# The first scan's values and gate columns become one product behind each row tile's transposes

## The chip, the cores and the metric

The kernel runs on one core of a Trainium2 chip. A core has a matrix engine (TensorE, PE in the profile, with its weight loads as PEld), a vector engine (VectorE, DVE), a scalar engine (ScalarE, ACT), a general one (GpSimd, POOL) and a queue engine (SyncE, SP) that issues the transfers here. The metric is the device time of one execution in microseconds. Three executions of the kernel before took 2996.06, 2998.18 and 3002.55 us, so the median is 2998.18. The profiled execution took 2996.87 us, and its span from the first to the last instruction is 2995.1 us.

## The reference

All arrays are fp32, with 1024 tokens of width 1024. A first block has two layers of the same form, each with three branches: a gated scan with four heads (GLA), a differential attention and a second gated scan (HGRN). A second block follows, with a neighbourhood attention and a delta rule; of it only small edits are touched. What the change touches in a layer is this.

```python
h = rms_norm(x, norm_pre[layer])
proj = h @ w_in[layer]
(gq, gk, gv, gg, gaf, gab, ...) = jnp.split(proj, offs, axis=-1)
# gla_branch:
v = split_heads(gv, GLA_HEADS)
lg_f = split_heads(jax.nn.log_sigmoid(gaf @ wa2_f + ba_f) / GLA_GATE_TEMP, GLA_HEADS)
lg_b = split_heads(jax.nn.log_sigmoid(gab @ wa2_b + ba_b) / GLA_GATE_TEMP, GLA_HEADS)
o = bidir_scan(q, k, k, v, lg_f, lg_b)
o = rms_norm(o, norm_w)
return merge_heads(o) * jax.nn.silu(g)
```

gq, gk are columns 0 to 255 of the projection, gv columns 256 to 511, gg 512 to 767, and gaf with gab the 32 columns 768 to 799.

## The kernel before

The tokens lie in 8 row tiles of 128. A product in fp32 is made of three products of fp32r parts: `split` gives H = the rounded value (a copy on ACT) and L = the rest (a subtraction, on VectorE unless another engine is named). So every product comes as HH, HL, LH over 8 blocks of the inner dimension: 24 matmuls an output tile.

A layer (`layer`, line 497 on) starts with its rows. In layer 0 each tile is loaded as x, squared on ACT with the sum (L307), gets its factor on GpSimd (L282, L283) and is multiplied by factor and norm row on VectorE (L312) into hn; in layer 1 the normed rows hn are loaded as they are. `transpose_split` (L287) turns each tile by 8 transposes in two PSUM tiles (tps) and splits it into hH and hL, which stay for the layer, as [channel, token].

Projections come in two forms. `proj_cm` is channel-major: weights are the stationary operand, 512 tokens the moving one, and the result has channels on its rows. `proj_tm` is token-major: a row tile's 128 tokens are stationary, the weights' columns move. Both write PSUM tiles pj, of which there are two. Weights come in pairs of 128 rows through two buffers wr and are split into wH, wL. Row tiles, channel-major results and gates live in ten buffers with the tag "in".

Projections are generators in a `Filler`, a list in the order in which they are due: gates (gf), queries and keys (gqk), values (gv), output gates (gg), and so on. `need` runs the list until a result is there; `run` steps a main computation and after each step gives the list a credit (RATE, in us), for which it emits matmuls beside it. Emission is also at a lower priority, and a scheduler lays out every engine's order when the program is built; each engine then works strictly in its order. SP's order is laid out in the same way, and at most 8 transfers are outstanding: an issue waits for the eighth before it.

The first scan needs gf and gqk. In `gla_gates` (L550) the 32 gate columns are projected channel-major (48 matmuls 32x512) into aT, multiplied with a small matrix (tile z), and go through Abs, Exp, Ln and Exp on ACT into the decay f. `scan_levels` (L340) forms running products of f, products psb and then six levels psl; `scan_finish` uses the values v. Constants of all stages are loaded early, the delta rule's bias dnb (dn_A_log, dn_dt_bias; L1275, L1286) too.

## Time and profile before

| what | us |
|---|---|
| median of three executions | 2998.18 |
| profiled execution | 2996.87 |
| its span | 2995.1 |
| TensorE busy | 2751.5 (92%) |
| VectorE busy | 1891.6 (63%) |
| ScalarE busy | 1228.9 (41%) |
| GpSimd busy | 555.2 (19%) |

A busy share is an average over stages with different limits. Where TensorE's share is below that of its neighbours, the timeline with its idle times says what it waited for. Matmuls overlap, so a step between two starts is what one costs, and not its listed duration. The granted clock of TensorE is 1.00 at 2.4 GHz and 0.5 at 1.2 GHz.

### The profile page before, as it was taken

The numbers are of one execution on the slowest core, as the hardware profiler recorded it, in microseconds if no ns is written. First come the engines' busy times: TensorE is split into PE (matmuls) and PEld (weight loads), VectorE is DVE, ScalarE is ACT, GpSimd is POOL, SyncE is SP. The second block draws the span as 40 slices with busy tenths as digits, with TensorE's granted clock in tenths as the row PEclk, the third lists the DMA queues.
The fourth block names the chain that finished last, engine by engine and source line by source line (L and its number), as shares of the span: only waits on it lengthen the run. The fifth ranks groups of instructions, "written<-read, shape, count | busy, mean of one in ns | idle before, by whom it ended". The sixth has DMA issues, their size and how long they took to land. (4 is left out here: it accounts for less than half of the span.)

```text
span 2995.1 us, 55723 instructions
## 1 busy us (share of the span) xinstructions
PE 2751.5 (92%) x21790; PEld 2342.9 (78%) x21790; DVE 1891.6 (63%) x4111; ACT 1228.9 (41%) x2729; POOL 555.2 (19%) x682
## 2 busy tenths in 40 slices
PE   7899889998999998899979899998899899989999
PEld 4788778896868886788968779875776677769889
DVE  4668777767546687766675645767686744346661
ACT  4232234556433322345564443433444433345430
POOL 1001212212100012222121212411422110010042
PEclk9999989998999998899989999998999999989999
DMA  3111122314331111223245534352435261255463
GB/s 112 29 43 36 41 79 79 94 48 120 128 142 30 44 36 41 78 80 102 53 132 160 180 88 135 119 137 57 132 107 145 78 172 45 71 151 149 145 206 97
DMA packets 355887, 293.61 MB, mean 98 GB/s; under 512 B 145798, under 2 KB 303110, under 8 KB 355624
## 3 DMA queue, kind: packets, MB, share of 16 engines
q1 hardware_dynamic: 355624, 290.04, 33.5%
q8 instruction: 172, 2.82, 0.4%
...
## 5 line engine op out<-in xcount | busy, mean ns | idle before, releaser
L163 DVE TENSOR_TENSOR wL<-wr,wH 128x512 fp32r<-128x512 f32 (+1 forms) x259 | 188.4, 733 | 216.5 <-ACT wH L162 213.5
L234 PE MATMUL pj<-wH,hH 128*128 128x256 f32 x1024 | 297.2, 292 | 14.8 <-ACT wH L162 8.5
L234 PE MATMUL pj<-wL,hH 128*128 128x256 f32 x1024 | 296.0, 290 | 1.2 <-DVE wL L163 1.2
L234 PE MATMUL pj<-wH,hL 128*128 128x256 f32 x1024 | 293.6, 288 | 0.0
L162 ACT CAST wH<-wr 128x512 fp32r<-128x512 f32 (+1 forms) x259 | 159.3, 618 | 277.8 <-PE pj L234 167.4
L234 PE MATMUL pj<-H,wH 128*128 128x512 f32 (+1 forms) x592 | 243.9, 414 | 8.8 <-DVE naz L1624 4.5
L234 PE MATMUL pj<-L,wH 128*128 128x512 f32 (+1 forms) x592 | 244.6, 413 | 0.0
L234 PE MATMUL pj<-H,wL 128*128 128x512 f32 (+1 forms) x592 | 244.5, 413 | 0.0
L234 PE MATMUL pj<-hH,wH 128*128 128x512 f32 (+1 forms) x544 | 221.5, 408 | 9.5 <-ACT raw L780 5.6
L234 PE MATMUL pj<-hL,wH 128*128 128x512 f32 (+1 forms) x544 | 222.3, 409 | 0.0
L282 POOL TENSOR_SCALAR rs<-ss 128x1 f32<-128x1 f32 (+2 forms) x190 | 68.9, 362 | 824.8 <-ACT sq L842 353.8
L234 PE MATMUL pj<-hH,wL 128*128 128x512 f32 (+1 forms) x544 | 221.5, 407 | 0.0
L234 PEld LDWEIGHTS pj<-wH,hH 128*128 128x128 f32 x1024 | 197.1, 193 | 20.6 <-ACT wH L162 9.9
L234 PEld LDWEIGHTS pj<-wL,hH 128*128 128x128 f32 x1024 | 197.6, 193 | 5.6 <-DVE wL L163 2.0
L234 PEld LDWEIGHTS pj<-wH,hL 128*128 128x128 f32 x1024 | 197.2, 193 | 2.6 <-issue 0.2
L814 DVE TENSOR_REDUCE nm<-psc 128x1 f32<-128x1024 f32 x128 | 155.6, 1219 | 43.1 <-PE psc L812 42.9
L817 ACT ACTIVATE p<-psc,nm 128x1024 f32<-128x1024 f32 x128 | 142.9, 1116 | 59.4 <-DVE nm L814 36.5
L283 POOL TENSOR_TENSOR rs<-rs,mhalf 128x1 f32<-128x1 f32 (+2 forms) x190 | 147.7, 778 | 15.3
L234 PEld LDWEIGHTS pj<-H,wH 128*128 128x128 f32 (+1 forms) x592 | 112.6, 190 | 35.8 <-DVE naz L1624 4.9
L839 PEld LDWEIGHTS pav<-v,wT 128*128 128x128 f32 x1024 | 132.0, 198 | 10.6 <-ACT wT L835 3.7
L839 PE MATMUL pav<-v,wT 128*128 128x128 f32 x1024 | 136.0, 282 | 2.5 <-ACT wT L835 2.0
L234 PEld LDWEIGHTS pj<-hH,wH 128*128 128x128 f32 (+1 forms) x544 | 101.8, 187 | 40.5 <-ACT raw L780 6.8
...
## 6 DMA issues: line engine op xcount, KB each, us to landing
...
xs<-raw SPq DMA_DIRECT2D x128, 64.0 KB
...
```

The costliest lines, as they stand in the source:

```text
L162: nc.scalar.copy(H, raw)
L163: (leng or nc.vector).tensor_tensor(L, raw, H.bitcast(F32), ALU.subtract)
L234: mm = k.nc.tensor.matmul(ps, x, y, start=i == 0, stop=i == len(terms) - 1)
L282: nc.gpsimd.tensor_scalar(r, ssq, scale, EPS, ALU.mult, ALU.add)
L283: nc.gpsimd.tensor_tensor(r, r, k.mhalf[:, :n], ALU.pow)
L814: nc.vector.tensor_reduce(nm, ps, axis=AX.X, op=ALU.max, negate=True)
L817: nc.scalar.activation(p, ps, AF.Exp, bias=nm, accum_out=z)
L839: k.mark = nc.tensor.matmul(po[:, :P], wT[:, kt, :], v[kt][:, vc0:vc0 + P], start=kt == 0, stop=kt == KT - 1)
```

## The change

The values and the gate columns of the first scan come from one token-major product with 288 columns, emitted right behind each row tile's transposes. Its weights sit in a new class that uses three buffers each of the tags "in" (low parts jL) and "be" (high parts jH). The result's 256 columns are copied to v, its 32 to ga; after four tiles four small transposes (tile aps) and a copy give half of aT. `gla_gates` is run directly, and no longer part of the list. In layer 0 rows are normed in place, and the squares go to a scratch tile jn. Constants' loads, and the first VectorE instruction on some of them, get an order-only dependency on the last weight load (lastw) or the last split of rows (lastL). The credit ahead of the first scan goes from 25.6 to 3.0. Several elementwise instructions move from GpSimd to VectorE, and one copy (sysA) from GpSimd to ACT.

```diff
@@ class Weights @@
-            nc.sync.dma_start(raw, src[i * P:(i + per) * P, :].rearrange(...))
+            k.lastw = nc.sync.dma_start(raw, src[i * P:(i + per) * P, :].rearrange(...))
+class JointWeights:
+    def __init__(self, k, src, n, src2, n2):
+        self.n = n + n2
+        self.L = [k.wk.tile([P, 3, self.n], F32R, tag="in", name="jL") for _ in range(3)]
+        self.H = [k.wk.tile([P, 3, self.n], F32R, tag="be", name="jH") for _ in range(3)]
+        raw2 = k.wp.tile([P, KT, n2], F32, tag="wr", name="wr")
+        nc.sync.dma_start(raw2, src2.rearrange("(k p) n -> p k n", p=P))
+        for i in range(3):
+            m = min(3, KT - 3 * i)
+            split(k, raw2[:, 3 * i:3 * i + m], self.H[i][:, 0:m, n:], self.L[i][:, 0:m, n:])
+        for k0 in range(0, KT, 2):
+            raw = k.wp.tile([P, 2, n], F32, tag="wr", name="wr")
+            k.lastw = nc.sync.dma_start(raw, src[k0 * P:(k0 + 2) * P, :].rearrange("(k p) n -> p k n", p=P))
+            ...
@@ transpose_split, behind, prenorm @@
-        nc.vector.tensor_tensor(L, pv, H.bitcast(F32), ALU.subtract)
+        k.lastL = nc.vector.tensor_tensor(L, pv, H.bitcast(F32), ALU.subtract)
+def behind(k, inst, mark):
+    info = mybir.DependencyInfo(mybir.DependencyClass.NoSync, mybir.DependencyReason.DATA)
+    k.tc.add_manual_dep(inst.ins, mark.ins.name, info, reason=...)
+    return inst
-    h = k.wk.tile([P, D], F32, tag="in", name="hn")
+    jk = k.wk.tile([P, D], F32, tag="at", name="jn")
-    nc.scalar.activation(h, x, AF.Square, accum_out=ss)
+    nc.scalar.activation(jk, x, AF.Square, accum_out=ss)
-        nc.vector.scalar_tensor_tensor(h, x, r, row, ALU.mult, ALU.mult)
+    nc.vector.scalar_tensor_tensor(x, x, r, row, ALU.mult, ALU.mult)
@@ scan_levels @@
-        nc.gpsimd.tensor_tensor(p0[:, :, 0, :], pf[:, :, 0, :], pb[:, :, 0, :], ALU.add)
-        nc.gpsimd.tensor_tensor(p1[:, :, 1, :], pf[:, :, 1, :], pb[:, :, 1, :], ALU.add)
+        nc.vector.tensor_tensor(p0[:, :, 0, :], pf[:, :, 0, :], pb[:, :, 0, :], ALU.add)
+        nc.vector.tensor_tensor(p1[:, :, 1, :], pf[:, :, 1, :], pb[:, :, 1, :], ALU.add)
@@ layer @@
-RATE = {"pre": 25.6, "gla": 4.95, ...}
+RATE = {"pre": 3.0, "gla": 4.95, ...}
+    def load_row(tt): ...
+    if l == 0:
+        load_row(0)
+        row = row_bcast(k, a["norm_pre"][l], D, k.wk, "in")
+        load_row(1)
+    Wv = JointWeights(k, w_in[:, 256:512], 256, w_in[:, 768:800], 32)
+    while len(hn) < NT:
+        load_row(len(hn))
+    ...
     for tt in range(NT):
+        if l == 0:
+            prenorm(k, hn[tt], row)
         transpose_split(k, hn[tt], tt // 4, tt % 4)
+        k.tc.cur_priority += RATE["low"]
+        ps = now(proj_tm(k, Wv, tt))
+        v = k.wk.tile([P, 256], F32, tag="v", name="v")
+        nc.scalar.copy(v, ps[:, 0:256])
+        gla_v.append(v)
+        ...
+        nc.scalar.copy(ga[:, tt % 4, :], ps[:, 256:288])
+        if tt % 4 == 3:
+            pt = k.sm.tile([P, 512], F32, tag="sm", name="aps")
+            for j in range(4):
+                nc.tensor.transpose(pt[:32, j * P:(j + 1) * P], ga[:, j, :], k.ident)
+            nc.scalar.copy(aT[:, tt // 4 * 512:tt // 4 * 512 + 512], pt[:32, :])
+        k.tc.cur_priority -= RATE["low"]
@@ gla_gates @@
-        Wa = Weights(k, w_in[:, 768:800], 32)
-        for half in range(2):
-            ps = yield from proj_cm(k, Wa, 0, 32, half)
-            nc.scalar.copy(aT[:, half * 512:half * 512 + 512], ps[:32, :])
@@ list and scan @@
-    F.add("gf", gla_gates())
-    F.add("gv", values(256))
-    fs = F.need("gf")
+    fs = gla_gates()
-    v, sg = F.need("gv"), F.need("gg")
+    v, sg = gla_v, F.need("gg")
@@ constants: every one in this form; lvlmask, bd4, bd2, lq, lk, lg, sc, modb, nw, nwc, rcos, rsin, wa, ba @@
-    nc.sync.dma_start(k.bd4, a["bd4"])
+    behind(k, nc.sync.dma_start(k.bd4, a["bd4"]), k.lastw)
-    nc.vector.tensor_scalar(th, th, 0.5, 0.5, ALU.mult, ALU.add)
+    behind(k, nc.vector.tensor_scalar(th, th, 0.5, 0.5, ALU.mult, ALU.add), k.lastL)
@@ second block @@
-        split(k, h.rearrange(...) if i == 0 else hv, H, L, nc.gpsimd if kt % 2 else nc.vector)
+        split(k, h.rearrange(...) if i == 0 else hv, H, L)
-    nc.gpsimd.tensor_copy(A, R.rearrange("s c r -> s r c"))
+    nc.scalar.copy(A, R.rearrange("s c r -> s r c"))
-        nc.gpsimd.tensor_tensor(e, e, D_.qT, ALU.mult)
+        nc.vector.tensor_tensor(e, e, D_.qT, ALU.mult)
-    nc.gpsimd.tensor_tensor(zv, zv, oT.rearrange(...), ALU.mult)
+    nc.vector.tensor_tensor(zv, zv, oT.rearrange(...), ALU.mult)
-    split(k, t, H, L, k.nc.gpsimd if c % 2 else k.nc.vector)
+    split(k, t, H, L)
-                nc.gpsimd.tensor_tensor(t, t, ut[:, hs], ALU.add)
+                nc.vector.tensor_tensor(t, t, ut[:, hs], ALU.add)
```

How the change moves the engines' orders is shown at three places. First TensorE at the very start of layer 0, in the kernel before; tps are a tile's transposes from the row tile hn, pj_311 is the gate columns' product:

```order
L294 MATMUL tps_188<-ident_60,hn_114 128x128 x4
L294 MATMUL tps_195<-ident_60,hn_114 128x128 x4
L294 MATMUL tps_202<-ident_60,hn_123 128x128 x4
L294 MATMUL tps_209<-ident_60,hn_123 128x128 x4
L294 MATMUL tps_216<-ident_60,hn_132 128x128 x4
L294 MATMUL tps_223<-ident_60,hn_132 128x128 x4
L294 MATMUL tps_230<-ident_60,hn_141 128x128 x4
L234 MATMUL pj_311<-hH_184,wH_306 32x512
L294 MATMUL tps_237<-ident_60,hn_141 128x128 x4
```

And in the changed kernel, where pj_186 is the first row tile's product with 288 columns:

```order
L320 MATMUL tps_172<-ident_60,hn_110 128x128 x4
L320 MATMUL tps_179<-ident_60,hn_110 128x128 x4
L260 MATMUL pj_186<-jH_119,hH_160 128x288
L260 MATMUL pj_186<-jL_116,hH_160 128x288
L320 MATMUL tps_222<-ident_60,hn_114 128x128 x4
L260 MATMUL pj_186<-jH_119,hL_162 128x288
L260 MATMUL pj_186<-jH_119,hH_160 128x288
L260 MATMUL pj_186<-jL_116,hH_160 128x288
L260 MATMUL pj_186<-jH_119,hL_162 128x288
L320 MATMUL tps_229<-ident_60,hn_114 128x128 x4
```

All tiles' transposes stood ahead of nearly all products; now the products of a tile stand between the transposes of the next ones.

Second, ACT between the casts of layer 0's first row tiles, in the kernel before; hn are the Squares (L307), hH_184 the casts of tiles 0 to 3, scth the Tanh of sc:

```order
L298 CAST hH_184<-tps_202 128x4x128
L307 ACTIVATE hn_150,ss_151<-x_148 128x1024
L298 CAST hH_184<-tps_209 128x4x128
L307 ACTIVATE hn_159,ss_160<-x_157 128x1024
L973 ACTIVATE scth_584<-sc_581 128x16
L298 CAST hH_184<-tps_216 128x4x128
L307 ACTIVATE hn_168,ss_169<-x_166 128x1024
L298 CAST hH_184<-tps_223 128x4x128
L878 ACTIVATE ls_543<-ls_543 128x2
L889 ACTIVATE lg_558<-lg_558 128x4
L162 CAST wH_403<-wr_401 128x512
L298 CAST hH_184<-tps_230 128x4x128
```

ACT in the changed kernel behind row tile 3 of layer 0: the copies of pj_285 and pj_334 are those of tiles 2 and 3, aT is the first half's gate columns, jn the Squares of tiles 4 to 7, and hH_161 their casts.

```order
L561 COPY ga_213<-pj_285 128x32
L162 CAST wH_627<-wr_625 128x512
L557 COPY v_359<-pj_334 128x256
L561 COPY ga_213<-pj_334 128x32
L1016 ACTIVATE scth_796<-sc_793 128x16
L566 COPY aT_164<-aps_362 32x512
L340 ACTIVATE jn_368,ss_369<-hn_152 128x1024
L340 ACTIVATE jn_418,ss_419<-hn_154 128x1024
L340 ACTIVATE jn_467,ss_468<-hn_156 128x1024
L340 ACTIVATE jn_516,ss_517<-hn_158 128x1024
L324 CAST hH_161<-tps_375 128x4x128
L324 CAST hH_161<-tps_382 128x4x128
```

TensorE's order at that place goes from tile 3's last products over the small transposes straight to tile 4:

```order
L260 MATMUL pj_334<-jL_118,hH_160 128x288
L260 MATMUL pj_334<-jH_121,hL_162 128x288
L565 MATMUL aps_362<-ident_60,ga_213 32x128 x3
L320 MATMUL tps_375<-ident_60,hn_152 128x128 x4
L320 MATMUL tps_382<-ident_60,hn_152 128x128 x4
L260 MATMUL pj_389<-jH_119,hH_161 128x288
```

The Squares of tiles 4 to 7 stood between the casts of tiles 0 to 3 before; now they stand behind everything of tile 3, and behind the Tanh of sc.

Third, the Exp of dn_A_log (dnb) and the gate chain on ACT. Before, in layer 0, between the Ln (L575) and the Exp (L578) of the second gate; cmt are copies of gqk:

```order
L597 ACTIVATE cmt_419<-pj_446 128x512
L575 ACT_TABLE_LOAD
L575 ACTIVATE fe_378<-fe_378 128x1024
L1286 ACT_TABLE_LOAD
L1286 ACTIVATE dnb_17519<-dnb_17519 128x8
L578 ACTIVATE f_377<-f_377 128x1024
L595 COPY cmt_472<-pj_473 128x512
```

In the changed kernel it stands in layer 1, between the casts hH of row tiles 0 and 1:

```order
L162 CAST jH_8497<-wr_8520 128x2x256
L324 CAST hH_8540<-tps_8552 128x4x128
L324 CAST hH_8540<-tps_8588 128x4x128
L162 CAST wH_8933<-wr_8931 128x512
L1329 ACTIVATE dnb_17463<-dnb_17463 128x8
L785 ACTIVATE xh_8470,ss2_8472<-o_8401 128x512
L324 CAST hH_8540<-tps_8595 128x4x128
L785 ACTIVATE xh_8471,ss2_8472<-o_8401 128x512
L557 COPY v_8584<-pj_8559 128x256
L561 COPY ga_8586<-pj_8559 128x32
```

And layer 0's gate chain in the changed kernel, with the copies of gqk between Ln and Exp (L620 is the Ln, L623 the Exp):

```order
L618 ACTIVATE fe_578<-fe_578 128x1024
L614 ACTIVATE fe_590<-z_591,ba_587 128x512
L620 ACT_TABLE_LOAD
L620 ACTIVATE fe_578<-fe_578 128x1024
L641 ACTIVATE cmt_631<-pj_632 128x512
L641 ACTIVATE cmt_631<-pj_658 128x512
L614 ACTIVATE fe_590<-z_595,ba_587 128x512
L623 ACT_TABLE_LOAD
L623 ACTIVATE f_577<-f_577 128x1024
```

beside TensorE's order there, where pj_685 is the third of gqk's four products and must have one of the two PSUM tiles back that pj_632 and pj_658 hold:

```order
L260 MATMUL pj_658<-hH_161,wL_628 128x512
L565 MATMUL aps_565<-ident_60,ga_416 32x128
L613 MATMUL z_583<-aT_164,wa_571 128x512
L613 MATMUL z_591<-aT_164,wa_571 128x512
L613 MATMUL z_595<-aT_164,wa_571 128x512
L260 MATMUL pj_685<-hH_160,wH_609 128x512
L260 MATMUL pj_685<-hL_162,wH_609 128x512
```

The dnb instruction left layer 0's gate chain for layer 1's rows, and the chain itself now stands around copies that free PSUM for the products behind them.

## Rows read from the trace of the kernel before

**Rows 1.** The first lines of the page: the span, and TensorE's busy time, its share of the span and its instructions.

```profile
span 2995.1 us, 55723 instructions
...
PE 2751.5 (92%) x21790; PEld 2342.9 (78%) x21790; DVE 1891.6 (63%) x4111; ACT 1228.9 (41%) x2729; POOL 555.2 (19%) x682
```

**Rows 2.** The sum of stages over layer 0's opening. Columns: the stretch from the span's start, its length, busy time and instructions of each engine, the granted TensorE clock, the busy share of the DMA engines, and GB/s.

```profile
0.00:26.70 26.70, 7.55 (x28) 5.15 (x28) 14.26 (x24) 14.40 (x28) 7.47 (x21) 1.00 0.78 223
26.70:62.00 35.30, 33.36 (x135) 19.50 (x136) 14.50 (x35) 16.32 (x25) 1.34 (x4) 1.00 0.21 60
62.00:86.00 24.00, 15.28 (x59) 11.27 (x57) 5.80 (x9) 8.81 (x12) 4.57 (x6) 0.81 0.06 12
86.00:111.00 25.00, 25.00 (x289) 24.41 (x292) 10.24 (x20) 7.67 (x12) 1.39 (x2) 0.85 0.16 44
```

**Rows 3.** The same sum over layer 1's opening.

```profile
855.00:893.00 38.00, 30.52 (x135) 19.28 (x134) 16.04 (x25) 13.72 (x27) 1.46 (x4) 0.82 0.16 58
893.00:914.00 21.00, 21.00 (x83) 15.10 (x83) 8.89 (x11) 16.07 (x18) 4.28 (x5) 1.00 0.10 28
```

**Rows 4.** TensorE in order of time: start, duration, line, operation, tile written from tiles read, and shapes. The first two products are gate columns at the low clock, the next two the same at the full one, then two of the values' product, then eight transposes.

```profile
30.00 0.63 PE L234 MATMUL pj<-hH,wH 128*32 128x512 f32 x1
30.43 0.63 PE L234 MATMUL pj<-hL,wH 128*32 128x512 f32 x1
...
48.45 0.39 PE L234 MATMUL pj<-hL,wH 128*32 128x512 f32 x1
48.68 0.40 PE L234 MATMUL pj<-hH,wL 128*32 128x512 f32 x1
...
104.98 0.28 PE L234 MATMUL pj<-wL,hH 128*128 128x256 f32 x1
105.09 0.28 PE L234 MATMUL pj<-wH,hL 128*128 128x256 f32 x1
...
874.63 1.06 PE L294 MATMUL tps<-ident,hn 128*128 128x128 f32 x8
```

**Rows 5.** Layer 0's opening by engine, in order of time (in brackets the idle time before and what ended it): the first Square, the first norm product, the first transposes, the first product, a copy of aT and a copy of values.

```profile
5.52 1.06 ACT L307 ACTIVATE hn<-x 128x1024 f32<-128x1024 f32 x1 [3.51 <-DMA x<-in_x_dram]
...
7.63 1.28 DVE L312 SCALAR_TENSOR_TENSOR hn<-x,rs,in 128x1024 f32<-128x1024 f32 x1 [7.63 <-POOL rs L283]
...
8.97 1.97 PE L294 MATMUL tps<-ident,hn 128*128 128x128 f32 x8 [8.97 <-DVE hn L312]
...
26.72 0.63 PE L234 MATMUL pj<-hH,wH 128*32 128x512 f32 x1 [2.69 <-ACT hH L298]
...
37.58 0.57 ACT L559 COPY aT<-pj 32x512 f32<-32x512 f32 x1
...
94.52 0.38 ACT L539 COPY v<-pj 128x256 f32<-128x256 f32 x1 [1.28 <-PE pj L234]
```

**Rows 6.** The wait before layer 0's scan: SP's issue of dn_A_log, ACT's wait, TensorE's wait and the first product for the scan (psb), then products of 256 columns.

```profile
69.60 1.29 SPq L1275 DMA_DIRECT2D dnb<-in_dn_A_log_dram  x2
...
81.00 1.28 ACT L1286 ACT_TABLE_LOAD   x1 [13.55 <-DMA dnb<-in_dn_A_log_dram]
...
84.49 0.58 PE L234 MATMUL pj<-wH,hH 128*128 128x256 f32 x1 [7.90 <-ACT wH L162]
85.90 1.51 PE L384 MATMUL psb<-cmt,K 32*128 32x64 f32 x21 [0.82 <-DVE K L374]
...
93.31 0.41 PE L234 MATMUL pj<-wH,hH 128*128 128x256 f32 x1
...
93.86 0.28 PE L234 MATMUL pj<-wH,hL 128*128 128x256 f32 x1
```

**Rows 7.** Layer 1's opening: SP's load of a row tile, the Abs and the last Exp of the gate chain on ACT, the first psb on TensorE.

```profile
856.22 0.32 SPq L512 DMA_DIRECT2D hn<-xh  x1
...
893.97 0.69 ACT L569 ACTIVATE fe<-z,ba 128x512 f32<-128x512 f32 x1 [1.39 <-PE z L568]
...
907.39 1.06 ACT L578 ACTIVATE f<-f 128x1024 f32<-128x1024 f32 x1
...
914.00 0.79 PE L384 MATMUL psb<-cmt,K 32*128 32x64 f32 x20
```

**Rows 8.** The sum of stages for 25 us in the levels of layer 0's first scan, columns as in rows 2.

```profile
125.00:150.00 25.00, 23.27 (x291) 21.94 (x291) 24.49 (x45) 1.92 (x5) 0.00 (x0) 1.00 0.02 6
```

**Rows 9.** The second issue for sc on SP, and the Tanh that reads sc on ACT.

```profile
15.23 1.77 SPq L971 DMA_DIRECT2D sc<-in_c_ctx_dram  x1
...
21.47 0.20 ACT L973 ACTIVATE scth<-sc 128x16 f32<-128x16 f32 x1
```

**Rows 10.** Groups of instructions of GpSimd and VectorE by line and shape: count, busy time, mean ns of one, and idle time before them with what ended it.

```profile
L1874 POOL TENSOR_TENSOR yt<-yt,ut 128x512 f32<-128x512 f32 x16 | 24.9, 1561 | 22.5 <-DVE yt L1873 7.6 <-ACT yH L162 5.2 <-DMA ut<-ud 3.9
...
L1511 POOL TENSOR_TENSOR qd<-qd,qT 128x1024 f32<-128x1024 f32 x8 | 20.4, 2554 | 50.8 <-ACT qd L1510 50.8
...
L163 DVE TENSOR_TENSOR L<-hf,H 128x512 fp32r<-128x512 f32 x8 | 5.5, 683 | 0.0
...
L1390 DVE TENSOR_TENSOR sysR<-sysR,sysb 128x1024 f32<-128x1024 f32 x5 | 6.1, 1221 | 0.0
...
L373 DVE TENSOR_TENSOR K<-cmt,f 128x256 f32<-128x256 f32 x4 | 3.3, 837 | 0.0
...
L373 DVE TENSOR_TENSOR K<-kx,f 128x256 f32<-128x256 f32 x8 | 3.2, 418 | 0.0
```

More of the change, by code (lines that the diff above doesn't have):

```diff
@@ L190, in part @@
         i, j = divmod(kt, self.per)
+        return self.H[i][:, j, :], self.L[i][:, j, :]
+class JointWeights:
+    def __init__(self, k, src, n, src2, n2):
+        nc = k.nc
+        self.n = n + n2
[9 more added lines that the diff above has]
+            k.lastw = nc.sync.dma_start(raw, src[k0 * P:(k0 + 2) * P, :].rearrange("(k p) n -> p k n", p=P))
+            for a, m in ((0, 2),) if k0 % 3 < 2 else ((0, 1), (1, 1)):
+                i, j = divmod(k0 + a, 3)
+                split(k, raw[:, a:a + m], self.H[i][:, j:j + m, 0:n], self.L[i][:, j:j + m, 0:n])
+    def part(self, kt):
+        i, j = divmod(kt, 3)
         return self.H[i][:, j, :], self.L[i][:, j, :]
@@ L298, in transpose_split, with prenorm @@
         nc.scalar.copy(H, pv)
-        nc.vector.tensor_tensor(L, pv, H.bitcast(F32), ALU.subtract)
-def prenorm(k, x, row=None):
+        k.lastL = nc.vector.tensor_tensor(L, pv, H.bitcast(F32), ALU.subtract)
+def behind(k, inst, mark):
+    info = mybir.DependencyInfo(mybir.DependencyClass.NoSync, mybir.DependencyReason.DATA)
+    k.tc.add_manual_dep(inst.ins, mark.ins.name, info, reason="constants come after the first rows and weights")
+    return inst
+def prenorm(k, x, row):
     nc = k.nc
-    h = k.wk.tile([P, D], F32, tag="in", name="hn")
+    jk = k.wk.tile([P, D], F32, tag="at", name="jn")
     ss = k.st.tile([P, 1], F32, tag="ss", name="ss")
-    nc.scalar.activation(h, x, AF.Square, accum_out=ss)
+    nc.scalar.activation(jk, x, AF.Square, accum_out=ss)
     r = rstd_of(k, ss, 1, 1.0 / D, k.st, "rs")
-    if row is None:
-        nc.vector.tensor_scalar_mul(h, x, r)
-    else:
-        nc.vector.scalar_tensor_tensor(h, x, r, row, ALU.mult, ALU.mult)
-    return h
+    nc.vector.scalar_tensor_tensor(x, x, r, row, ALU.mult, ALU.mult)
 def row_bcast(k, src, n, pool, tag):
@@ L324, in col @@
     t = pool.tile([P, 1], F32, tag=tag, name=tag)
-    k.nc.sync.dma_start(t, src.rearrange("(p o) -> p o", o=1))
+    behind(k, k.nc.sync.dma_start(t, src.rearrange("(p o) -> p o", o=1)), k.lastw)
     return t
```

69 lines of the change are left out of this document (33 added, 36 removed).

## The prediction

> **What bounds the kernel now.** I began with the page's first part: TensorE is busy 2751.5 of 2995.1 us, so about 244 us stand idle on it [rows 1]. A sum of stages was next: time is lost where a layer opens. In layer 0's first 111 us TensorE is idle for 19.1, 1.9, 8.7 and 0 us in four stretches, and the granted clock is 0.81 and 0.85 in the last two; in layer 1 the stretch 855 to 893 loses 7.5 us to idleness at a clock of 0.82, and from 893 on nothing [rows 2, 3]. Elsewhere TensorE is nearly full, so there a gain must be instructions taken from TensorE; in the openings it must be a wait that ends earlier.
>
> The timeline then shows what ends those waits. In layer 0 the first row tile is squared at 5.52 and its transposes begin at 8.97 [rows 5]; the first product begins at 26.7, because weights and rows fill the DMA engines (78% busy, 223 GB/s) [rows 2]. Later ACT stands 13.55 us for a load of dn_A_log that was issued at 69.60 and came at about 80.9; TensorE waits 7.90 us behind that, and after it runs at half the steps' speed until 93.9 [rows 6].
>
> **Products.** TensorE's step between two products is 0.23 us for 512 columns and 0.117 for 256; at the low clock the 512 columns take 0.43 [rows 4]. The change removes 48 products 32x512 (11.2 us) and 192 of 128x256 (22.4) from a layer, and adds 192 of 288 columns. No row has 288 columns; between the 256 and 512 of rows 4 lies the proportional 0.131, the bounds are 0.117 (no dearer than 256) and 0.15. I take 0.131, as 512 cost twice 256: 25.2 us, and 0.9 for eight small transposes (eight take 1.06 with the last one's tail [rows 4], 0.11 apart). So 7.5 us a layer go; 4 to 10 by the bounds. All of them stand on TensorE, the bounding engine, so this part counts in full as long as no new wait opens.
>
> **Layer 0's opening.** What TensorE loses in the first 111 us before: up to 26.7 it does 28 transposes, 3.1 us at full clock, and loses 23.6; then 1.9 idle and 2.7 for the 5.4 us in which the steps are 0.43; 8.7 idle and 24 x 0.19 = 4.6 by the clock; 25 x 0.15 = 3.8 by the clock [rows 2, 4]. Sum 45.3 us. After, by the same account:
> a. The products behind tile 0 need all four weight pairs; SP issues them between the row tiles, the last after x of tile 6. That is 5.2 MB; at 223 GB/s 23.4 us, with the first issue and the split 26. By then four tiles are transposed (3.5 us) and three quarters of two tiles' products done (4.7); only two PSUM banks take products, so a third tile can't begin. Lost 17.8 (15 to 20).
> b. The low clock at the start of steady work: 2.7, as before.
> c. Behind tile 3 ACT's order has the copies of v and gates, the Tanh of sc, the copy of aT, and only then the Squares of tiles 4 to 7, and TensorE has nothing between. Copies 0.6 (v's takes 0.38), Tanh 0.2, small transposes 0.3 and aT 0.57, then 3.45 from a Square's start to its tile's first transpose [rows 5]: 5.1, with hand-overs 5.5. The three further Squares keep ACT from tile 4's cast by another 1.5. The low clock that follows cost 4.7 in rows 6 (9.4 us at half speed after 7.90 us idle); I take 4. Together 11, between 3 (waits beside other products) and 15. The Tanh waits for sc, whose issue is now behind the fourth weight of gqk; before, it was issued at 15.23 to 17.0 and used at 21.47 [rows 9], and by a sum of sizes it is now issued near 27, so it has landed by 35, when ACT comes to it.
> d. The gates: from the first Abs of one half in layer 1 to the last Exp's end is 14.5 us and to the first psb 20.0 [rows 7], while filler kept TensorE full. Now only two of gqk's four products (11.2 us) are left to stand beside it, and the third must wait for a PSUM bank that is emptied by an ACT copy behind Abs, Exp, table load and Ln. Lost 8 (3 to 12). The load of dn_A_log is no longer in this place, so its 13.55 us go.
> Sum 17.8 + 2.7 + 11 + 8 = 39.5. Layer 0 gains 7.5 + 45.3 - 39.5 = 13.3 us, between 3 and 23 by the bounds. The lower credit ahead of the scan (3.0 for 25.6) only moves filler behind it; TensorE stays full there or VectorE sets the pace (24.49 of 25 us between 125 and 150 [rows 8]), and I count nothing for it.
>
> The clock's price is weighed once more, since it speaks against the change. The Trainium skill ("TensorE: Matmul & The Clock Gate", Terms) says that what the throttle costs is the time spent throttled times the missing share of the clock. Rows 6 agree: 9.4 us at half are 4.7. By that rule each of the new waits c and d would be paid twice, once idle and once slow, and with 4.7 behind d as well layer 0 would gain 8.6 for 13.3, and the time be 2988.
>
> **Layer 1's opening.** Before, 7.5 us idle and 38 x 0.18 = 6.8 by the clock, 14.3 [rows 3]. After: the Exp of dn_A_log now stands in ACT's order between the casts of tile 1. Its loads stand on SP behind the load of row tile 5, which in the trace before went at 856.22, when the output projection had left its buffer [rows 7]. With some 11.3 us from issue to landing, as in rows 6, it lands near 868.5; casts and products wait on ACT from about 862, less 3 us of tile 0's products still in hand. I take 7 (0 to 12) with 4.5 of low clock. Queued behind it on ACT are the cast of tile 1's second half, the copies of v, and so both PSUM banks. Early gaps 2.8, d as in layer 0: 8. Sum 22.3; layer 1 gains 7.5 + 14.3 - 22.3 = -0.5, between -9 and +11 (no wait for dn_A_log, d 5).
>
> **GpSimd's work to VectorE.** 24 adds of the scans, 8 qd, 4 zl, 16 yt and 16 splits leave GpSimd (qd 2.55, yt 1.56 us each) and cost VectorE about 48 us: 256 columns 0.42, 512 columns 0.68, 1024 columns 1.22 [rows 10], so 24 x 0.42, 12 x 1.22, 16 x 0.68, and for the splits 8 x 0.68, 4 x 0.42, 4 x 1.22. VectorE is off the path in most places: it is busy 63%. Part comes back: a product of VectorE beside GpSimd's add took 0.837 (K from cmt), with none beside it 0.418 (K from kx) [rows 10]; 8 to 16 such give 3 to 7 us. What waited for GpSimd were only yH behind yt, while TensorE was fed by others. I take +2 us, bounds -40 and +7.
>
> The Trainium skill ("GPSIMD Engine Reference", 4.1 Engine selection) gives two-input elementwise work to VectorE, with GpSimd about twice as slow. yt agrees, 1.56 by 0.68 [rows 10]; qd's 2.55 by 1.22 too. By this rule the edit frees some 50 us of engine time; were half of that on the path, the time would be 2958, but no row shows GpSimd there.
>
> **Sum.** 13.3 - 0.5 + 2 = 14.8 us less than the profiled execution's 2996.87: 2982. The three runs' median is 1.3 above the profiled one, so 2983.
>
> **Rivals.**
> B, the openings give it all back. In c the idle time is 11 with 4 behind it, a is 20, d 12: 52.8 - 49.7 = 3 in layer 0; layer 1 -4; rest 0: 2998. For it: ACT runs in order, and three late things (Squares, Ln, dn_A_log) stand ahead of what TensorE waits for. Against: the biggest wait of before goes in any case.
> C, no clock is lost and no late load: c 7, d 3: 52.8 - 30.5 = 22.3; layer 1 +11; rest +4: 2961. For it: in layer 1 before, ACT's waits for the gate chain left TensorE full. Against: then it had 192 products of filler, and has gqk alone now.
> D, VectorE becomes the bound, and the time is longer. Place: the levels, where VectorE is already 98% busy [rows 8], the second block's delta phase and the end of the merge. Price up to 48 - 7 = 41 us; it decides when over 19 of these are on the path (it then has eaten the 13 and 6 more); at 20 the time is 3005. For it: the levels' row. Against: the adds of a scan come ahead of its levels, where VectorE had waits, and in the second block TensorE is the fuller engine.
>
> **How the numbers follow.** My forecast 0.50, its own range 2972 to 2992 (the 11 and 8 of c and d, and layer 1's 7, by some 10 together). B 0.20, C 0.18, D 0.12. The range for 8 in 10 goes from C's 2961 to just under D's 3005: 2961 to 3004. No change is what lies within 0.2%, 6 us, about what a measurement of this kernel can tell. Faster by more: 0.49 of the forecast, C's 0.18, 0.04 of B: 0.71. Same: 0.12 of B, 0.03 of the others: 0.15. Slower: D's 0.11 and 0.03 of B: 0.14.
>
> **What would show it.** Per layer 48 products 32x512 and 192 of 256 fewer and 192 of 288 columns at a step of 0.131. In layer 0 the first product near 13, tile 0's last near 26, an idle stretch of 5 to 8 us on TensorE behind tile 3 ended by VectorE's hn, one of 5 to 8 ahead of the first psb, which comes near 96 (26, 36 of products and transposes left ahead of the gates, b and c, 20 of chain), and no wait of 13 us for dn_A_log there, but one of 4 to 11 us on ACT between 858 and 872. If GpSimd's part matters, K's products take 0.42 everywhere, and VectorE's idle time in the levels is below before's. The forecast is wrong if tile 4's transposes follow tile 3's products at once, if dn_A_log has landed when ACT comes to it, or if the levels of a scan take longer than before.

## The result and the profile after

The changed kernel took 2977.9 us (median of 4 runs, 2971.94 to 2978.88), the kernel before 2999.33 on the same chip: ratio 0.9924, interval 0.9907 to 0.9942. That is 21 us less where the forecast had 15, and 2977.9 lies inside the forecast's own range of 2972 to 2992. The total came out, but by luck: the sum took nearly all of the gain from the openings and 2 us from the work that left GpSimd, and the runs below show that this work alone brings some 25 and that the openings add nothing to it. The profiled execution is the lowest of the four, 2971.94.

The page's first lines, which answer to [rows 1]:

```profile
span 2969.8 us, 55512 instructions
...
PE 2732.9 (92%) x21710; PEld 2341.8 (79%) x21710; DVE 1897.2 (64%) x4185; ACT 1238.1 (42%) x2756; POOL 437.7 (15%) x609
```

TensorE's busy time fell by 18.6 us. VectorE's rose by 5.6, though some 48 us of work came to it; GpSimd's fell by 117.5.

Layer 0's opening by stages, columns as in [rows 2]:

```profile
0.00:26.70 26.70, 15.50 (x93) 13.92 (x94) 14.00 (x22) 14.97 (x31) 3.67 (x15) 1.00 0.74 244
26.70:62.00 35.30, 27.33 (x177) 24.93 (x176) 15.37 (x36) 13.67 (x32) 6.32 (x10) 0.85 0.32 76
62.00:86.00 24.00, 17.52 (x61) 11.53 (x60) 4.33 (x9) 9.08 (x14) 2.21 (x3) 0.81 0.04 9
86.00:111.00 25.00, 24.59 (x276) 21.64 (x275) 17.58 (x35) 14.40 (x19) 0.95 (x1) 0.98 0.16 43
```

Up to 26.7 TensorE is now busy 15.50 us for 7.55, since products run between the transposes. Then it loses: 8.0 idle and 15% of the clock in 26.7 to 62, 6.5 idle and 19% of the clock in 62 to 86. What ended its longest waits there (start, duration, engine, line, operation, tiles and shape; in brackets the idle time and what ended it):

```profile
37.95 1.97 PE L320 MATMUL tps<-ident,hn 128*128 128x128 f32 x8 [5.49 <-DVE hn L342]
...
42.73 1.12 PE L320 MATMUL tps<-ident,hn 128*128 128x128 f32 x4 [2.15 <-DVE hL L325]
...
79.26 2.07 PE L613 MATMUL z<-aT,wa 32*128 32x512 f32 x2 [3.49 <-DVE f L615]
83.21 0.80 PE L260 MATMUL pj<-hH,wH 128*128 128x512 f32 x1 [1.88 <-ACT cmt L641]
```

The first two are the wait behind row tile 3, the third stands ahead of the last two z, the fourth is gqk's third product behind the copies that free its PSUM tile. ACT's order in the same opening:

```profile
24.37 0.37 ACT L557 COPY v<-pj 128x256 f32<-128x256 f32 x1 [0.56 <-PE pj L260]
...
33.93 0.22 ACT L1016 ACTIVATE scth<-sc 128x16 f32<-128x16 f32 x1 [1.81 <-DMA sc<-in_c_ctx_dram]
...
34.52 1.05 ACT L340 ACTIVATE jn<-hn 128x1024 f32<-128x1024 f32 x1
...
37.65 1.04 ACT L340 ACTIVATE jn<-hn 128x1024 f32<-128x1024 f32 x1
```

Tile 0's values are copied at 24.37, so its product ended near 24.3; the Tanh waits 1.81 us for sc, and the four Squares follow it. On VectorE stands a wait that the prediction had not seen:

```profile
77.94 0.29 DVE L918 TENSOR_TENSOR lq<-lq,lk 128x128 f32<-128x128 f32 x1 [16.93 <-DMA lk<-in_diff_lk_dram]
...
78.47 0.74 DVE L615 TENSOR_SCALAR f<-z,ba 128x512 f32<-128x512 f32 x1
```

The product lq x lk waits 16.93 us for lk; the minimum of L615, which frees the PSUM tile of a z, is queued behind it. The table of waits of SP's queue over the first 110 us names the cause (who waited, for whom: us in total, times, longest):

```profile
SPq L917 <- PE aps L565: 33.6, 1, 33.6
```

lk's load (L917) waits 33.6 us for the transposes aps, because lk takes a buffer of the tag bd, and ga, the new tile of gate columns, which the transposes aps read, holds it.

Layer 1's opening, by stages (they answer to [rows 3]):

```profile
840.50:893.00 52.50, 37.16 (x262) 34.94 (x260) 17.83 (x29) 18.57 (x45) 1.93 (x6) 0.84 0.29 90
893.00:926.00 33.00, 28.95 (x110) 20.83 (x109) 9.33 (x14) 16.84 (x21) 2.85 (x3) 0.90 0.01 1
```

and what stands in it, SP's issue of dn_A_log, ACT's Exp of it, and TensorE's wait:

```profile
843.45 5.09 SPq L1318 DMA_DIRECT2D dnb<-in_dn_A_log_dram  x2
```

```profile
862.10 0.21 ACT L1329 ACTIVATE dnb<-dnb 128x8 f32<-128x8 f32 x1 [17.32 <-DMA dnb<-in_dn_A_log_dram]
```

```profile
863.45 0.61 PE L260 MATMUL pj<-jH,hH 128*128 128x288 f32 x1 [14.27 <-ACT hH L324]
```

ACT stands 17.32 us for a load issued at 843.45, TensorE 14.27. The first psb comes 85.5 us behind the output projection's end (840.5 to 926.0) for 59.0 before.

The products of 288 columns have a step of 0.13 us:

```profile
53.13 0.29 PE L260 MATMUL pj<-jL,hH 128*128 128x288 f32 x1
53.26 0.29 PE L260 MATMUL pj<-jH,hL 128*128 128x288 f32 x1
```

And VectorE's groups, which answer to [rows 10]: count, busy time, mean ns, idle time before.

```profile
L163 DVE TENSOR_TENSOR wL<-wr,wH 128x512 fp32r<-128x512 f32 x248 | 174.1, 705 | 162.7 <-ACT wH L162 151.1 <-PE pkt L470 3.6 <-PE psb L413 2.8
...
L1917 DVE TENSOR_TENSOR yt<-yt,ut 128x512 f32<-128x512 f32 x16 | 11.0, 686 | 1.0 <-DMA ut<-ud 0.9
...
L1554 DVE TENSOR_TENSOR qd<-qd,qT 128x1024 f32<-128x1024 f32 x8 | 9.8, 1223 | 5.6 <-ACT qd L1553 5.6
...
L402 DVE TENSOR_TENSOR K<-cmt,f 128x256 f32<-128x256 f32 x4 | 1.7, 420 | 0.0
```

yt and qd take 0.69 and 1.22 us where GpSimd took 1.56 and 2.55, and K's product, which VectorE had before too, 0.42 for 0.837.

For reading several profiles side by side, the times of the same events on TensorE, from the timelines of all runs below (us from the span's start; psb and psl are the scans' products, psc the attention's first scores, pout the output projection; the last column is the length of the second block, from the end of layer 1's last output product to the end of the last pf):

| kernel | first psb | scan 2, first psl | first score psc | layer 0, last pout | layer 1, first psb | layer 1, last pout | second block |
|---|---|---|---|---|---|---|---|
| before | 85.9 | 248.1 | 420.5 | 855.0 | 914.0 | 1674.3 | 1316.2 |
| before, once more | 86.3 | 250.6 | 421.1 | 855.3 | 914.0 | 1674.6 | 1322.4 |
| changed | 96.5 | 226.0 | 398.8 | 840.5 | 926.0 | 1664.0 | 1301.2 |
| pool_back | 96.6 | 227.1 | 410.7 | 851.4 | 936.5 | 1686.1 | 1319.3 |
| pool_only | 87.0 | 248.6 | 409.0 | 850.1 | 909.8 | 1672.7 | 1296.6 |
| delta_moves | 86.1 | 248.5 | 418.3 | 854.4 | 913.4 | 1673.8 | 1315.6 |
| sysA_act | 86.7 | 249.2 | 420.6 | 852.2 | 912.1 | 1674.1 | 1322.3 |
| k_adds | 85.6 | 247.2 | 406.4 | 851.7 | 910.4 | 1674.0 | 1311.8 |
| opening_k | 96.0 | 225.8 | 399.2 | 840.0 | 924.3 | 1664.1 | 1315.1 |
| opening_fixed | 91.1 | 225.6 | 410.7 | 845.9 | 913.9 | 1665.3 | 1333.9 |
| ga_own | 91.5 | 220.8 | 400.8 | 833.9 | 918.0 | 1659.8 | 1306.7 |
| dnb_late | 96.6 | 225.7 | 399.7 | 840.9 | 909.5 | 1647.8 | 1305.2 |
| all_fixed | 90.3 | 220.5 | 399.4 | 834.2 | 902.1 | 1645.0 | 1319.8 |
| dnb_mid | 91.1 | 220.4 | 400.6 | 836.0 | 904.1 | 1645.5 | 1297.8 |

By this table the changed kernel gains 14.5 us in layer 0, loses 4.2 in layer 1 and gains 15 to 21 in the second block. In the two layers, delta_moves and sysA_act run every engine in the same order as the kernel before, so these two rows and the first two show the spread there: 3 us at the end of layer 0, and 0.8 at the end of layer 1.

### The profile page after: what moved, and what is told of

It is laid out like the page before. It is cut to its first block, busy times and chain, and to the rows that moved or that the text cites. A ratio compares the mean times of both kernels' runs of the same rounds, so it can differ in the third digit from the quotient of the medians.

```text
span 2969.8 us, 55512 instructions
## 1 busy us (share of the span) xinstructions
PE 2732.9 (92%) x21710; PEld 2341.8 (79%) x21710; DVE 1897.2 (64%) x4185; ACT 1238.1 (42%) x2756; POOL 437.7 (15%) x609
## 5 line engine op out<-in xcount | busy, mean ns | idle before, releaser
L260 PE MATMUL pj<-wH,hH 128*128 128x256 f32 x896 | 259.7, 292 | 8.1 <-ACT raw L823 6.0
L260 PE MATMUL pj<-wL,hH 128*128 128x256 f32 x896 | 260.1, 291 | 3.5 <-DVE wL L163 3.4
L260 PE MATMUL pj<-wH,hL 128*128 128x256 f32 x896 | 257.2, 288 | 0.0
L260 PE MATMUL pj<-hH,wH 128*128 128x512 f32 x512 | 209.5, 409 | 5.5 <-ACT cmt L641 4.1
L260 PE MATMUL pj<-hL,wH 128*128 128x512 f32 x512 | 208.1, 406 | 0.0
L260 PE MATMUL pj<-hH,wL 128*128 128x512 f32 x512 | 207.8, 406 | 0.0
L260 PEld LDWEIGHTS pj<-wH,hH 128*128 128x128 f32 x896 | 172.5, 193 | 13.0 <-ACT raw L823 6.9
L260 PEld LDWEIGHTS pj<-wL,hH 128*128 128x128 f32 x896 | 173.2, 193 | 7.9 <-DVE wL L163 4.5
L260 PEld LDWEIGHTS pj<-wH,hL 128*128 128x128 f32 x896 | 172.8, 193 | 2.5 <-issue 0.5
L260 PEld LDWEIGHTS pj<-L,wH 128*128 128x128 f32 (+1 forms) x592 | 111.7, 189 | 25.1 <-DVE L L163 0.2
```

What stands on the lines that cost most here:

```text
L260: mm = k.nc.tensor.matmul(ps, x, y, start=i == 0, stop=i == len(terms) - 1)
```

## The experiments

Each ratio is against runs of the kernel before on the same chip, whose medians there were 3003 to 3004.

**A second profile of the kernel before (before_again).** The kernel, unchanged.

> The kernel before, word for word, for a second profile. Theory: profiles of one kernel agree within 1 us up to the end of layer 1 and differ by up to 8 at the end, so the differences of profiles in the layers can be read, those in the delta phase only by medians. Rival: they differ by several us in the layers too, and then no difference of two profiles under 5 us counts. Ratio 1.000 within its interval.

Ratio 0.9998 (0.9988 to 1.0009). In the layers the two profiles differ by at most 2.5 us (more than the 1 us expected, at scan 2), at the end of layer 1 by 0.3, and over the whole span by 6.5:

```profile
span 3001.6 us, 55723 instructions
```

So differences of profiles in the layers can be read above some 3 us; in the second block only above some 7, and there the medians decide.

**All moved work back on GpSimd (pool_back).**

```diff
-        nc.vector.tensor_tensor(p0[:, :, 0, :], pf[:, :, 0, :], pb[:, :, 0, :], ALU.add)
+        nc.gpsimd.tensor_tensor(p0[:, :, 0, :], pf[:, :, 0, :], pb[:, :, 0, :], ALU.add)
```

and the same for the other lines of the diff that name GpSimd or sysA. In the layers K's adds are all that moves; the rest lies in the second block.

> The changed kernel with all that moved from GpSimd put back on GpSimd (K's adds, the splits, qd, zl, yt, the copy sysA). Theory 1: of the 21 us gained, some 14 lie behind the layers, where only these moves act, so this runs near 2992. Rival: the moves are neutral, as the prediction's +2 had it, and the 14 us come from a new order or from run to run; then it runs near 2978 to 2980.

3012.89, ratio 1.0033 (1.0021 to 1.0044): not 2992, but 10 us slower than the kernel before. What is left of the change, the openings with the late constants and the lower credit, costs time by itself. Theory 1 had the direction and too small a size, since it looked behind the layers alone: by the table 22 us are lost in the layers, where K's adds are back on GpSimd, and 18 behind them. The last pout of layer 1 comes at 1686.1, 11.8 behind the kernel before, while the second block is as long as there.

**Only the moves from GpSimd (pool_only).** The kernel before with the opposite edit.

> The kernel before with only the moves from GpSimd to VectorE and ACT. Theory 1: it gains some 14 us, 2985. Rival (moves neutral): 2997 to 3000. Rival D of the prediction (VectorE becomes the bound): above 3005.

2974.44, ratio 0.9916 (0.9892 to 0.9941): all of the gain of the change, and rival D is out. Its page, and VectorE's groups, first in the kernel before, then here:

```profile
span 2973.9 us, 55680 instructions
...
PE 2743.1 (92%) x21790; PEld 2334.8 (79%) x21790; DVE 1905.7 (64%) x4179; ACT 1239.8 (42%) x2734; POOL 443.2 (15%) x609
```

```profile
L163 DVE TENSOR_TENSOR wL<-wr,wH 128x512 fp32r<-128x512 f32 x256 | 186.9, 735 | 216.1 <-ACT wH L162 213.2 <-PE pj L234 1.7
...
L1347 DVE TENSOR_TENSOR A<-A,gc 128x1024 f32<-128x1024 f32 x8 | 12.3, 1537 | 4.8 <-DMA A<-gc_d 4.8
```

```profile
L163 DVE TENSOR_TENSOR wL<-wr,wH 128x512 fp32r<-128x512 f32 x256 | 178.5, 701 | 189.6 <-ACT wH L162 184.1 <-DMA Tm<-r_d 2.1 <-PE pj L234 1.7
...
L1347 DVE TENSOR_TENSOR A<-A,gc 128x1024 f32<-128x1024 f32 x8 | 9.8, 1219 | 0.4 <-DMA A<-gc_d 0.4
...
L373 DVE TENSOR_TENSOR K<-cmt,f 128x256 f32<-128x256 f32 x4 | 1.7, 420 | 0.0
```

VectorE is busy 1905.7 us, 14.1 more than before, though the 73 moved instructions, less the 5 copies that went to ACT, bring it some 48: 34 us have come back from other instructions of its own. The mean of the 256 splits wL fell from 735 to 701 ns, of A from 1537 to 1219, of K's product from 837 to 420.

A mean hides how this comes about. One instruction of VectorE, the same line and shape, in the kernel before, and what ran on GpSimd beside its first and its second showing:

```profile
214.31 0.42 DVE L374 TENSOR_TENSOR K<-kx,f 128x256 f32<-128x256 f32 x1
...
217.86 1.09 DVE L374 TENSOR_TENSOR K<-kx,f 128x256 f32<-128x256 f32 x1
```

```profile
213.94 0.96 POOL L350 MEMSET B<- 128x1024 f32 x1 [3.25 <-PE pkt L441]
...
217.81 0.85 POOL L372 TENSOR_TENSOR K<-kx 128x256 f32<-128x256 f32 x1
```

Beside a memset the product takes 0.42 us, beside an add of two inputs 1.09. In the same trace the 206 splits wL with nothing on GpSimd beside them took 690 ns on average (671 to 737), and the 24 beside a two-input instruction of GpSimd's of 256 columns or more 1103. So it is a few long ones that raise the mean, and they are long because of what ran beside them.

**Three moves of the delta phase alone (delta_moves).**

```diff
-        nc.gpsimd.tensor_tensor(e, e, D_.qT, ALU.mult)
+        nc.vector.tensor_tensor(e, e, D_.qT, ALU.mult)
-    nc.gpsimd.tensor_tensor(zv, zv, oT.rearrange(...), ALU.mult)
+    nc.vector.tensor_tensor(zv, zv, oT.rearrange(...), ALU.mult)
-    nc.gpsimd.tensor_copy(A, R.rearrange("s c r -> s r c"))
+    nc.scalar.copy(A, R.rearrange("s c r -> s r c"))
```

> The kernel before with three of the moves alone: qd and zl to VectorE, the copy sysA to ACT (all in the delta phase). The moves of all engines' work alone took 25 us from the kernel before; its first scans and layers gave 2, the delta phase 24. Theory: GpSimd's 2.0 to 2.5 us instructions stand in the delta phase's chain, and this alone gains 15 to 24 us of the kernel before beside it. Rival: the order around them changed by chance; then less than 6 us.

2988.92, ratio 0.9961 (0.9948 to 0.9975), 12 us less, somewhat under the theory's 15, above the rival's 6. This rests on the times of ten executions; the profiled one (2995.78, the second longest of them) shows little of it, with 1315.6 us in the second block for 1316.2 and 1322.4.

**The copy sysA alone (sysA_act).** The last pair of lines above.

> The kernel before with the copy sysA alone moved from GpSimd to ACT (5 copies of 2.12 us). Theory: the copy stands in the solve's chain, and most of the 12 us of the three delta moves come from it: 6 us or more. Rival: qd and zl carry it, 24 and 10 us of GpSimd's time beside VectorE's chain; then within 3 us of the kernel before.

3004.77, ratio 1.0007 (0.9996 to 1.0018). The theory falls: the copy carries nothing, so the 12 us lie with qd and zl, or with the order that came with them. Which of the two carries them was not run.

**K's adds alone (k_adds).** The kernel before with the opposite of the first diff above.

> The kernel before with only K's adds on VectorE. Theory: little, 0 to 4 us, since they stand ahead of the levels. Rival (VectorE bounds the levels): slower by 3 or more. Rival (any change of order moves the phases by 10 us): gain or loss beyond 6.

2989.22, ratio 0.9951 (0.9934 to 0.9967): 14 to 15 us where 0 to 4 were expected, and beyond the 6 at which the second rival, a change of order, is met. Its profile shows 3.3 us at the end of layer 0 and 0.3 at the end of layer 1; where the rest of the median's gain lies, one profile can't tell, since its execution (2992.14) is the slowest of its four. The order did change: on TensorE the second block departs from the kernel before's within its first 200 matmuls, though nothing there was edited. So the adds and the new order aren't told apart, and this stays open.

**The openings with K's adds (opening_k).** The changed kernel with the second block's moves undone.

> The changed kernel with the second block's moves undone, K's adds still on VectorE: the openings and K's adds. Theory: what the openings gain is spent in scans that VectorE and GpSimd pace, and K's adds give it back, so the two together give more than their sum: 2988 to 2994. Rival (they add: +10 and -14): 2997 to 3001.

2989.54, ratio 0.9945 (0.9930 to 0.9959), as the theory had it: more than the sum of 10 lost and 15 gained. But K's adds alone had 0.9951, so beside them the openings neither cost nor bring anything that the times show. Between scan 2's first psl and the first score this kernel needs 173.4 us, the one with K's adds on GpSimd 183.6. What TensorE waits for in that stretch, first with the adds on GpSimd:

```profile
PE psl L436 <- DVE Kt L429: 8.0, 5, 6.8
PE pj L260 <- ACT raw L823: 6.9, 2, 5.0
```

```profile
227.10:410.70 183.60, 159.51 (x1314) 139.43 (x1314) 139.66 (x285) 50.67 (x106) 37.24 (x34) 0.92 0.18 46
```

then with the adds on VectorE:

```profile
PE pj L260 <- ACT raw L823: 1.3, 1, 1.3
...
PE psl L436 <- DVE Kt L429: 0.8, 1, 0.8
```

```profile
225.80:399.20 173.40, 156.19 (x1313) 136.82 (x1313) 134.81 (x282) 49.36 (x105) 29.67 (x30) 0.95 0.18 46
```

With the adds on GpSimd TensorE waits 8.0 us for Kt (0.8 with them on VectorE) and 6.9 for raw (1.3), and its clock is 0.92 (0.95). Other waits go the other way, so its idle time falls by 6.9 us in all, from 24.1 to 17.2. So the lead over the kernel before with which scan 2 begins, 21.0 and 22.3 us, shrinks to 9.8 in the one and stays 21.3 in the other.

**ga in the buffers of another tag (ga_own).**

```diff
-            ga = k.wk.tile([P, 4, 32], F32, tag="bd", name="ga")
+            ga = k.wk.tile([P, 4, 32], F32, tag="y", name="ga")
```

> The changed kernel with the gate columns' tile ga in the buffers of tag y, not in those of bd that lq and lk use. Theory: the load of lk no longer waits 33.6 us for ga's buffer, VectorE's 16.9 us wait ahead of the gates goes, TensorE's 3.92 us before the last two z go, and the first psb comes 3 to 5 us earlier: 2974. Rival: ACT's chain Abs, Exp, Ln, Exp sets the first psb and the time stays within 1.5 us of 2978.

2970.43, ratio 0.9894 (0.9875 to 0.9912), 9 us below what the changed kernel's ratio gives. The loads of lk now go at 29.27 and 30.22, and VectorE's wait is 3.02 us and earlier:

```profile
29.27 0.43 SPq L917 DMA_DIRECT2D lk<-in_diff_lk_dram  x1
...
30.22 0.43 SPq L917 DMA_DIRECT2D lk<-in_diff_lk_dram  x1
```

```profile
60.26 0.29 DVE L918 TENSOR_TENSOR lq<-lq,lk 128x128 f32<-128x128 f32 x1 [3.02 <-DMA lk<-in_diff_lk_dram]
```

TensorE's wait ahead of the last two z is 0.71 us for 3.49, and the first psb comes at 91.5, 5.0 earlier, at the top of what was expected.

**dn_A_log behind the second block's weights (dnb_late).**

```diff
-            nc.sync.dma_start(t[h * 64:h * 64 + 64, :], src[:, h].partition_broadcast(64))
+            behind(k, nc.sync.dma_start(t[h * 64:h * 64 + 64, :], src[:, h].partition_broadcast(64)), k.lastw)
```

> The changed kernel with the loads of dn_A_log and dn_dt_bias ordered behind the last weight load issued before the delta phase, so that its Exp leaves layer 1's opening. Theory: ACT's 17.32 us wait and TensorE's 14.28 us go, less what the row tiles' own loads still cost; the first psb of layer 1 comes 10 to 15 us earlier and the time is 2963 to 2969. Rival: the gate chain behind it is what ends late in any case, and less than 4 us are gained (2974 or more).

2963.11, ratio 0.9874 (0.9854 to 0.9894), 15 us below the changed kernel's ratio. Layer 1's first psb comes 16.5 us earlier. But the wait has moved to where the second block opens:

```profile
1694.83 0.21 ACT L1329 ACTIVATE dnb<-dnb 128x8 f32<-128x8 f32 x1 [10.21 <-DMA dnb<-in_dn_A_log_dram]
```

```profile
1698.36 1.11 PE L1116 MATMUL tps<-ident,hx 128*128 128x128 f32 x4 [10.54 <-DVE hf L1122]
```

**Both, and gqk's copies on VectorE (all_fixed).**

```diff
-    F.add("gqk", cm_tile(0, 256, [lambda d, s_: nc.scalar.activation(d, s_, AF.Copy, scale=32 ** -0.5), copy]))
+    F.add("gqk", cm_tile(0, 256, [lambda d, s_: nc.vector.tensor_scalar_mul(d, s_, 32 ** -0.5), lambda d, s_: nc.vector.tensor_copy(d, s_)]))
```

> The changed kernel with dn_A_log's loads late, ga in the buffers of y, and gqk's copies on VectorE, which has 17 us of waiting there. Theory: the first two add up (15 and 8), the third takes the 1.9 us wait of the third product in each layer: 2950 to 2956 where the changed kernel has 2978. Rival: they overlap, since dn_A_log's loads late already free the queue: 2960 to 2963.

2965.84 (2953.04 to 2971.18), ratio 0.9859 (0.9829 to 0.9889). The median lies above both, and the interval, about 2952 to 2970 us, takes in all of the rival's range and most of the theory's, so neither the sum nor the third edit is settled. The wait at the second block's opening is in this kernel too, 12.03 us on ACT.

**The openings without their two new waits, all moved work on GpSimd (opening_fixed).** The diffs of pool_back, ga_own and dnb_late together.

> The changed kernel with all moved work back on GpSimd, and with the two new waits of its openings taken away (dn_A_log's loads behind the last weight load, ga in the buffers of y). The opening as it was made ran 10 us slower than the kernel before. Theory: the two waits cost it 15 and 5 to 7 us, so this is 8 to 14 us faster than the kernel before. Rival: what the openings gain is given back in the attention phases whatever stands before them; then within 4 us of the kernel before.

3001.99, ratio 0.9987 (0.9975 to 1.0000). The time is the rival's, but its cause isn't what the profile shows. The layers end 9 us ahead of the kernel before, as the theory's 8 to 14 had it, so the attention doesn't take it all. What takes it is that the wait for dn_A_log is not gone but moved to the second block's opening:

```profile
1716.47 0.21 ACT L1329 ACTIVATE dnb<-dnb 128x8 f32<-128x8 f32 x1 [13.51 <-DMA dnb<-in_dn_A_log_dram]
```

```profile
1717.76 1.06 PE L260 MATMUL pj<-H,wH 128*32 128x512 f32 x2 [11.16 <-ACT H L162]
```

TensorE stands 11.16 us there, and the second block is 12 to 18 us longer than before. What the openings bring with neither wait and all moved work on GpSimd was not run.

**dn_A_log in layer 1's attention, its Exp behind the last output rows, ga in y (dnb_mid).**

```diff
+        k.lastw1 = k.lastw
         out = output(k, l, xin, xout)
-            nc.scalar.activation(xh[i], o[:, hs[i]], AF.Square, accum_out=s2[:, i:i + 1])
+            k.lastA = nc.scalar.activation(xh[i], o[:, hs[i]], AF.Square, accum_out=s2[:, i:i + 1])
-            nc.sync.dma_start(t[h * 64:h * 64 + 64, :], src[:, h].partition_broadcast(64))
+            behind(k, nc.sync.dma_start(t[h * 64:h * 64 + 64, :], src[:, h].partition_broadcast(64)), k.lastw1)
-    nc.scalar.activation(al, al, AF.Exp)
+    behind(k, nc.scalar.activation(al, al, AF.Exp), k.lastA)
```

> The changed kernel with ga in the buffers of y, dn_A_log's loads ordered behind layer 1's last projection weight, and its Exp behind the last Squares of layer 1's output. With the loads behind the second block's weights ACT waited 10.2 us for them and TensorE 10.54 where that block opens. Theory: here neither place waits, so it beats the changed kernel by 15 (layer 1), 8 (ga) and the 10 given back: 2945 to 2957 beside 2978. Rival: the gains overlap as in the kernel with three edits, and it stays at 2963 or above.

2953.05 (2950.06 to 2956.28), ratio 0.9825 (0.9812 to 0.9837): 51 us less than the kernel before, 25 to 30 less than the changed one. ACT waits for dn_A_log nowhere:

```profile
1652.58 0.20 ACT L1330 ACTIVATE dnb<-dnb 128x8 f32<-128x8 f32 x1
```

```profile
span 2947.9 us, 55533 instructions
...
PE 2724.2 (92%) x21710; PEld 2331.4 (79%) x21710; DVE 1894.1 (64%) x4185; ACT 1237.5 (42%) x2756; POOL 442.2 (15%) x609
```

Its ratio is 0.9825 where the moves of work alone have 0.9916, so once neither wait is in them, the openings bring some 27 us beside the moves.

**Is it the work that moved, or the order?** A new order of the second block came with nearly every edit, also where nothing in that block was touched, so it is a rival to each of them. For the moves taken together the table speaks against it: with the second block's work left on GpSimd (before twice, sysA_act but for its copy, k_adds, opening_k, pool_back) that block took 1312 to 1322 us, in five orders; with all of it moved (pool_only, changed, ga_own, dnb_mid) 1297 to 1307, in four. The three kernels with the moved wait fit in when TensorE's wait is taken off: opening_fixed 1323, dnb_late 1295, all_fixed 1308 (its wait is 11.46 us). For K's adds alone, and for qd and zl alone, the rival isn't excluded.

## Why the prediction was right, point by point

**The total.** It came out by luck. Forecast were 12.8 us from the two layers and 2 from the work that left GpSimd. The moves of work by themselves take the kernel to 0.9916 and the whole change to 0.9924, so the 21 us are theirs, and the openings add nothing to them as long as their two new waits stand (0.9825 without, in dnb_mid).

**The products.** Right: 0.13 us for 288 columns, and 18.6 us less of TensorE's busy time by the page, 7.5 a layer forecast.

**Layer 0's opening.** Up to the first psb the account is right: 39.6 us lost, forecast 39.5, and each term near its own. a: by 26.7 us 32 transposes and 61 products had begun, 11.5 us of work at their steps, so 15.2 were lost, forecast 17.8; tile 0's product ends near 24.3 for 26. b and c: between 26.7 and 62 TensorE idles for 8.0, of which 5.49 end by VectorE's hn (forecast 5.5) and 2.15 by a split (1.5), and the clock of 0.85 over 35.3 us takes 5.3; together 13.3, forecast 2.7 and 11. That sc would be there when ACT comes to it was wrong by 1.81 us. d: 6.5 idle between 62 and 86, of which 3.49 and 1.88 in the rows shown, and 4.6 by the clock of 0.81 there, so 11 for 8. So the clock fell at c and at d both, as in the prediction's other reckoning of it, which left layer 0 a gain of 8.6. Of the 3.49 the forecast knew nothing: it had followed the constants past SP's queue and not past their buffers, and lk's buffer is held by ga. The first psb comes at 96.5, forecast near 96. Layer 0 gains 14.5 us by its last pout, forecast 13.3; but with K's adds back on GpSimd the same opening, its first psb at 96.6, gains 3.6.

**Layer 1's opening.** The mechanism is right and its size off: ACT's wait is 17.32 us and TensorE's 14.27, where the sum has 7 within 0 to 12. Counted from layer 0's end (855.0 before, 840.5 now), ACT came to the Exp after 4.3 us, forecast 7, and the load was there after 21.6, forecast 13.5. It went some 3 us behind that end and took 18.7 from its issue, for the 11.3 of [rows 6]; the two issues held SP for 5.09 us, for 1.29 there. Layer 1 loses 4.2 us, forecast 0.5, and without the wait it is 16.6 us shorter, as dnb_late's rows of the table show.

**GpSimd's work to VectorE.** This step failed: "I take +2 us, bounds -40 and +7". The two terms that it added up were what VectorE pays (48, right) and what comes back (3 to 7 from K's products alone; these gave 7). Measured, 34 us came back, because other instructions of VectorE's were long beside GpSimd's as well, those of two inputs above all: the splits wL gave back 9 us, the 8 of A 2.5. So VectorE got 14 us more work and not 41. The prediction's row of 0.418 "with none beside it" is a product beside a memset or an operation of one column, not beside an idle GpSimd; what counts is that no large two-input instruction ran there. The moves alone are worth 25 us, the whole gain of the change. By which way they act, through VectorE's shorter instructions or through GpSimd's own in some chain, is not shown: in the two profiles of the kernel before no matmul of the second block waits for GpSimd, just as the prediction had it that no row shows GpSimd on the path, and yet qd and zl bring 12 us by the times.

The Trainium skill ("GPSIMD Engine Reference", 1. Specifications) says that GpSimd shares its SBUF interfaces with VectorE, with contention for VectorE's instructions with two SBUF inputs; this trace agrees, 837 to 420 ns for K's product and 1537 to 1219 for A. The reckoning that the prediction weighed and set aside, half of some 50 us of engine time, gave the moves 25 us, which is what they bring alone; but the half was a guess, and its total of 2958 has the openings' 12.8 in it, which did not come.

**How the two meet.** The second step that failed is that what the openings gain reaches the end of the layers and adds to the moves; of the stages behind the opening the prediction says "I count nothing for it". By the ratios the openings alone cost 10 us, K's adds alone gain 15, both together 16.5; the moves alone gain 25, with the openings 23. In the layers the table shows the same: openings alone end them 11.8 us later, K's adds alone 0.3 earlier, both 10.2 earlier. So the 10.3 us by which the changed kernel's layers end earlier need K's adds off GpSimd; with them there, scans 2 and 3 of layer 0 give back 11 us, in part in waits for Kt and raw, and layer 1, with its new wait, runs 15 longer than before. That the forecast 12.8 for the layers is near 10.3 is thus luck in the cause, though the waits of layer 0 were forecast near their sizes. And of these 10 us the times show nothing beside the moves; the second block gives back 3 to 5 of them by the profiles (opening_k beside k_adds, the changed kernel beside pool_only), and the rest stays open.

**Rival B** (the openings give it back) describes what they do by themselves, with 3.6 us in layer 0 for its 3; its place was wrong, since the loss lies behind them, in the scans, and in layer 1's wait. **Rival D** is out: from the first to the last psl of scan 1 the levels take 76.9 us before, 77.1 with the moves alone and 65.5 in the changed kernel. **Rival C's** 2961 was passed only when both new waits were gone (dnb_mid, 2953).

What stays open: where K's adds gain 14 to 15 us by the times, of which their profile shows 5 to 11; by which way qd and zl gain 12; and the moves of the merge and of the splits, which were not tried alone.
